# One recurrence for all four head pairs instead of two, and an output projection in one PSUM sum per tile

## The chip, the cores and the metric

The kernel runs on one core of a Trainium2 chip. The metric is the time of one execution on the device, in microseconds (us).

## The reference

One layer of a hybrid decoder: two SwiGLU feed-forward blocks, and between them a mixing layer of RWKV-7 heads beside a short convolution. A prompt of 512 tokens and 8 requests of 4 tokens go through it together.

```python
x = layer_norm(ALPHA * x + 0.5 * swiglu(x, ffn1...), ln1)
proj = x @ w_in                           # 3328 columns
r, k, v, wd, ad, gd = shift_mix(proj[:1792])
# 8 heads of 64; for each token
sa = S @ (-kk)
S  = S * w + outer(sa, kk * a) + outer(v, k)
o  = S @ r
y_rwkv = (group_norm(o) + sum(r * k * r_k) * v) * g
y_conv = c_b * conv3(c_c * c_h)
x = layer_norm(ALPHA * x + concat(y_rwkv, y_conv) @ w_out, ln2)
x = layer_norm(ALPHA * x + 0.5 * swiglu(x, ffn2...), ln3)
# outputs: x, and the last S, shift and conv rows of prompt and requests
```

## The kernel before, in words

**Layout.** Model dimensions lie on the 128 partitions, the T = 544 tokens (512 and 8 x 4) on the columns, cut into two halves of 256 and 288 (`HALF`). Each large product is made of three matmuls on split operands (`mm3`, lines L180, L181, L182); weights come from HBM as `raw` and are split into `hl` by ACT (L160) and DVE (L161).

**Fill.** The kernel records its instructions in one order by hand. Long products (input projection of the convolution, `conv`; output projection, `wout0`, `last0`, `wout1`) are generators in a background list, and `weave`, `slots`, `take` and `gap` put so many ns of them between the small matmuls of the recurrence. The table `FILL` gives those amounts. I call an L180/181/182 matmul in this part "fill". The order on each engine is thus fixed before it runs: an instruction that waits holds up everything behind it on its engine, and on the SP queue, which issues most of the DMAs.

**Recurrence.** The 8 heads are 4 pairs; two pairs are a group (g = 0: pairs 0 and 1, g = 1: pairs 2 and 3). The prompt is 8 chunks of 64 tokens, the requests are a ninth. For each pair, `scores` multiplies the scaled r, k, kk against each other (L1156) into `SC`, masks it (L1159), transposes what the chain needs and writes the matrix to be inverted to DRAM (`Ad`, L1163, SP). For each group:
- `elim(g)`: the 16x16 blocks on the diagonals are read back to the layout of one block per partition (`AT`, L1219), inverted on DVE in 15 steps of a multiply (L1230) and an add (L1232), written to DRAM (`Dd`, L1235 and L1236) and read back to the matmul layout (`DM` and `DT`, L1239). `DT` lies in `O`'s memory.
- `rounds(g)`: four rounds of 64-row matmuls (L1269) make the 64x64 inverses from the 16x16 ones.
- `chain(g)`: for chunk after chunk W (L1333, copied by ACT L1336), u (L1342), the state's product (L1351) with its update on DVE, and the outputs (L1312, L1318). The requests (`sample`: L1405, L1420, L1427, L1436, L1445) are put between.
- `gnorm(g, h)`: the norm of the outputs of a token half (L1463), gate (L1485).

The order in the program is scores of pairs 0 and 1, `elim(0)`, rounds, chain, norm; scores of 2 and 3, `elim(1)`, rounds, chain, norm. Group 0's result goes through DRAM (`ycd`).

**Output projection.** The sum over 8 blocks of 128 runs in two PSUM sums for the first token half: blocks 0, 1 and the convolution's 4 to 7 during chain 1 (`wout0`), blocks 2 and 3 behind it (`last0`), each added into `z` by DVE. The second half (`wout1`) has parts in one sum. Weights that both halves use are loaded and split twice.

**First layer norm.** The sums of squares over the 8 blocks are added by POOL for one token half (L344, L346; `add_sum`), the rest by DVE.

Of the kernel before, what the change touches and what calls it, by code (L numbers as in the profile page):

```python
# [67 lines left out]
FILL = dict(l1a=1.1, l1b=0.8, p0=11900, s0=0.93, p1=5506, s1=1.832, e0=0.658, c0=0.233, g0=0.399, g1=0.8, s2=0.531, p3=425, s3=0.85, e1=0.392, c1=0.963, c2=0.734, c3=0.8, l2a=0.94, l2b=1.25, l3a=0.88)  # L68
# [14 lines left out]
def body(ctx: ExitStack, tc: tile.TileContext, xT, gu1, wd1, win, wo_c, wo_0, wo_1, gu2, wd2, wl, ln3, eye, lora, vec, cst,  # L83
# [118 lines left out]
    def slots(gen, run):  # L202


        while True:
            with ExitStack() as st:
                if seen["fill"] is not None:
                    st.enter_context(tc.issue_after(seen["fill"].ins))
                if next(gen, None) is None:
                    break  # L210
            with ExitStack() as st:
                for e in [seen["pe"]] + seen["old"]:
                    st.enter_context(tc.issue_after(e.ins))
                take(run)
            seen["old"], seen["new"] = seen["new"], []
        seen["old"] = []
# [819 lines left out]
    SC = tl([P, 2, 2, NC_, P], F32, name="SC")  # L1036
    BK = tl([P, 2, 2, 8, 64], F32, name="BK")
    UV = tl([P, 2, 2, NC_, 64], F32, name="UV")
    XT = tl([P, NC_, 2, 64], F32, name="XT")
    DM = tl([P, NC_, 2, 64], F32, name="DM")  # L1040
    O = tl([P, 2, NC_, 64], F32, name="O")
    DT = O.rearrange("p a b t -> p (a b t)")[:, 0:1024].rearrange("p (c d t) -> p c d t", c=8, d=2)
    Pe = tl([P, 4, 8], F32, name="Pe")
    Pes = tl([P, 4, NSEQ], F32, name="Pes")
    ast = ExitStack()
    ARs = [(tl if g else pool(ast, "ar0").tile)([P, 2, NC_, 2, 64], F32, name=f"AR{g}") for g in (0, 1)]
    bvs = [[tl([P, 576], F32, name=f"bv{g}{pl}") for pl in range(2)] for g in range(2)]
    kfs = (kf, bvs[1][1]) * 2
    POOL.memset(bvs[1][1][:, T:576], 0.0)
    POOL.memset(XT, 0.0)  # L1050
    UP = tl([P, 2, 64], F32, name="UP")
    BS = tl([P, 2, P], F32, name="BS")
    POOL.memset(BS, 0.0)
    Ad = dr.tile([2, 16, 65, 64], F32, name="Ad")
    Dd = [dr.tile([2, 16, 65, 64], F32, name=f"Dd{i}") for i in range(2)]
    for d in Dd:
        for par in range(2):
            dma(d[par, :, 0:64].rearrange("c s t -> s c t"), XT[R(par), 0:8].rearrange("p c d t -> p (c d) t"))
    SEG = ((0, 256, 0), (256, 576, 1))

    class Pair:
# [79 lines left out]
        def scores(self):  # L1141
            p, pl, bkb, nk, vf = self.p, self.pl, self.bkb, self.nk, self.v

# [7 lines left out]
            AR, bv = ARs[p // 2], bvs[p // 2]  # L1151
# [13 lines left out]
            for a0c, n in ((0, 5), (5, 4)):  # L1165
# [8 lines left out]
                for par, q in enumerate(qs):  # L1174
                    src, dst = s64(q[:, :64 * m]), BK[:, pl, par, a0c:a0c + m, :]
                    if p == 2 and not a0c:
                        DVE.tensor_copy(dst, src)
                    else:
                        ACT.activation(dst, src, AF.Copy)
# [23 lines left out]
            for t0, t1, _ in SEG:  # L1203
# [3 lines left out]
                DVE.tensor_tensor(bv[pl][:, t0:t1], vf[:, t0:t1], q[:, :t1 - t0], op=OP.mult)  # L1207
# [4 lines left out]
    def elim(g, mid=None):  # L1212
        AR = ARs[g]
        est = ExitStack()
        ep = pool(est, f"elim{g}")
        AT = ep.tile([P, 16, 16], F32, name="AT")
        De = ep.tile([P, 16, 16], F32, name="De")
        tm = ep.tile([P, 64], F32, name="tm")
        dma(AT, diag(Ad))  # L1219
        POOL.memset(De, 0.0)  # L1220
        POOL.memset(De.rearrange("p a b -> p (a b)")[:, 0:256:17], 1.0)
        for pl in range(2):
            for par in range(2):
                sc = SC[R(par), pl, par, 0:8, 0:64]
                DVE.tensor_tensor(sc, sc, offm[R(par), None, :].to_broadcast([64, 8, 64]), op=OP.mult)
        yield 3000
        for k in range(15):
            n = 15 - k
            tv = tm[:, :n * (k + 1)].rearrange("p (i j) -> p i j", j=k + 1)
            DVE.tensor_tensor(tv, AT[:, k, k + 1:16, None].to_broadcast([P, n, k + 1]),  # L1230
                              De[:, k, None, 0:k + 1].to_broadcast([P, n, k + 1]), op=OP.mult)
# [5 lines left out]
        for d, x in zip(Dd, (DM[:, 0:8], DT)):  # L1237
            for par in range(2):
                dma(x[R(par)].rearrange("p c d t -> p (c d) t"), d[par, :, 0:64].rearrange("c s t -> s c t"))  # L1239
        est.close()  # L1240
        if mid is not None:
            mid()
        yield 24000 if g else 0

    def rounds(g):
        AR = ARs[g]
        pieces = (range(0, 4), range(4, 8), range(8, 9))
        for rnd in range(4):
            for x in pieces:
                sam = x[0] == 8  # L1250
                m = (64, 64, 32, 16)[rnd]
# [5 lines left out]
                for c in x:  # L1257
                    for pl in range(2):
                        for par in range(2):
# [3 lines left out]
                            lhs = DM[pr, c, pl, 0:m] if rnd else SC[pr, pl, par, c, 0:m]  # L1263
                            rhs = (DM if rnd == 0 else DT if rnd == 1 else XT) if not sam else XT
                            if sam and rnd < 2:
                                rhs = ident[pr, 0:32]
                            else:
                                rhs = rhs[pr, c, pl, j0:j0 + nn]
# [3 lines left out]
                if rnd == 0:  # L1272
                    for pr in (slice(0, 32), slice(64, 96)) if sam else (slice(0, P),):
                        ACT.activation(DM[pr, cc, :, 0:nn], qv[pr], AF.Copy)
                    continue
                elif rnd == 1 and not sam:
                    DVE.tensor_copy(XT[:, cc, :, 0:16], DT[:, cc, :, 0:16])
                    DVE.tensor_tensor(XT[:, cc, :, 16:64], qv, DT[:, cc, :, 16:64], op=OP.add)
                    continue
                for par in range(2):  # L1280
                    pr = slice(64 * par, 64 * par + m)
                    dst = XT[pr, cc, :, j0:j0 + nn]
# [6 lines left out]
            if rnd == 0:  # L1289
                for pl in range(2):  # L1290
                    for par in range(2):
                        POOL.tensor_copy(SC[R(par), pl, par, 0:8, 0:64], AR[R(par), pl, 0:8, 0, :])
# [5 lines left out]
    def chain(g, cp, small):  # L1298
# [3 lines left out]
        AR = ARs[g]  # L1302
        heads = [(pl, par) for pl in range(2) for par in range(2)]
        Ss, q2, uv = {}, None, []
# [4 lines left out]
        def out_u(c):  # L1309
            q = sm()  # L1310
            for pl, par in heads:
                crit(PE.matmul(at(q, pl, par), UV[:, pl, par, c, :], SC[:, pl, par, c, 64:128], start=(pl == 0 or c == 0),  # L1312
                               stop=(c == 0), skip_group_check=True))
            return q

        def out_s(c, q):
            for pl, par in heads if c else ():
                crit(PE.matmul(at(q, pl, par), Ss[c][R(par), pl, par, :], AR[R(par), pl, c, 1, :], start=False, stop=True,  # L1318
                               skip_group_check=True))
            o = ACT.activation(O[:, :, c, :], v2(q), AF.Copy)  # L1320
            for e in uv:
                after(o, e)

        for c in range(8):
            if c < 7:
                Sn = Ss[c + 1] = tl([P, 2, 2, 64], F32, name="S", bufs=3)
# [3 lines left out]
            q = sm()  # L1330
            for pl, par in heads:
                k = slice(0, P) if c else R(1 - par)
                crit(PE.matmul(at(q, pl, par), SC[k, pl, par, c, 0:64], Ss[c][:, pl, par, :] if c else UV[k, pl, par, c, :],  # L1333
                               start=True, stop=True))
            W = tl([P, 2, 64], F32, name="W", bufs=2)
            ACT.activation(W, v2(q), AF.Copy)  # L1336
            if c:
                q2 = out_u(c - 1)
            small(c, 0)
            qs = (sm(), sm())  # L1340
            for pl, par in heads:
                crit(PE.matmul(at(qs[par], pl, par), XT[R(par), c, pl, :], W[R(par), pl, :], start=True, stop=True))  # L1342
            seen["uv"] = DVE.tensor_copy(UV[R(0), :, 0, c, :], v2(qs[0], R(0)))
            seen["new"] = [ACT.copy(UV[R(1), :, 1, c, :], v2(qs[1], R(1)))]
            uv[:] = seen["new"]
            if c:
                out_s(c - 1, q2)
            small(c, 1)
            q = sm()
# [13 lines left out]
            if not g:  # L1363
                seen["step"] = upd, uv[0]
            small(c, 2)
            if c == 7:
                dma(wkvp_o[:, 2 * g:2 * g + 2, :], SF)
                out_s(7, out_u(7))
            yield 1

    def recur(g, cp, run):
        sam, gn = sample(g, cp), gnorm(g, 0, cp)
        first = (2, 2) if g else (1, 1)
        when = {first: 1, (2, 0): 1, (2, 1): 1, (3, 0): 1, (3, 1): 1, (4, 2): 1, (5, 2): 2, (6 if g else 7, 2): 2}

        gaps = {(0, 0): 600, (0, 1): 600, (1, 1): 300, (4, 0): 300, (4, 1): 300, (7, 0): 300, (7, 1): 300}

        def small(c, k):
            for _ in range(when.get((c, k), 0)):
                next(sam, None)  # L1380
            if (c, k) in gaps:
                gap(gaps[c, k])
            if (c, k) in ((5, 0), (5, 1), (6, 0)):
                next(gn, None)

        seen["fine"] = True
        slots(chain(g, cp, small), run)
        seen["fine"] = False
        for x in (sam, gn):
            for _ in x:  # L1390
# [513 lines left out]
```

## Time and profile before

| | |
|---|---|
| time, median of 3 runs | 1051.78 us (1051.11 to 1053.48) |
| the profiled execution's own time | 1052.82 us |
| its span, first to last instruction | 1051.1 us |
| PE busy | 1036.1 us of the span |
| DVE busy | 842.7 us |
| ACT busy | 602.5 us |
| POOL busy | 161.0 us |
| mean granted TensorE clock | 0.997 |

Matmuls are pipelined, so their durations overlap: a row's duration is from start to end of one (280 to 290 ns for a fill matmul), and what it costs the engine is the distance from its start to the next start. The trace has two records for one of the recurrence's 32-bit matmuls, which the program order lists once; counts below are those of the trace unless they are called the order's.

### The profile page before, as it was taken

The page shows a single profiled execution, that of the slowest core. Times are in us where ns is not written, and L with a number is a line of the kernel's source. Part 1 is how long each engine was busy: PE and PEld are TensorE (multiplying, and loading weights), DVE is VectorE, ACT ScalarE, POOL GpSimd, SP SyncE. Part 2 cuts the span into 40 slices and gives each one's busy share as a digit, 9 for nine tenths or more (in the row PEclk, how much of TensorE's full clock was granted, in tenths as well). Part 3 has the DMA queues.
Part 4 walks back from the last instruction along what each step waited for, and adds up shares of the span by engine and source line. Part 5 has one row for each costly group of instructions (what it writes and reads, how often), then busy time and mean ns, then how long its engine had stood idle before and what let it go on. Part 6 is the DMA issues. An engine that isn't in the chain of part 4 may idle for free.

```text
span 1051.1 us, 22674 instructions
## 1 busy us (share of the span) xinstructions
PE 1036.1 (99%) x9162; PEld 1004.3 (96%) x9162; DVE 842.7 (80%) x1521; ACT 602.5 (57%) x1155; POOL 161.0 (15%) x279
## 2 busy tenths in 40 slices
PE   9999999999999999999999999999999999999997
PEld 8999999999999899899889988999999999999995
DVE  6897988889775886896587668999889798897656
ACT  5765656565553569655454544677566565565514
POOL 0211111212100222123000200002112121120000
PEclk9999999999999999999999999999999999999999
DMA  8556676766745133325135744334667767686512
GB/s 295 137 135 148 152 183 149 163 161 152 171 120 162 61 106 94 95 73 122 43 106 168 176 127 147 131 120 99 144 161 161 162 142 175 148 180 162 141 44 85
DMA packets 91529, 144.49 MB, mean 137 GB/s; under 512 B 34848, under 2 KB 52384, under 8 KB 91296
## 3 DMA queue, kind: packets, MB, share of 16 engines
q1 hardware_dynamic: 68144, 110.76, 34.5%
q0 software_dynamic: 22848, 31.72, 19.4%
q8 instruction: 72, 1.18, 0.5%
q10 hardware_dynamic: 432, 0.56, 0.2%
q14 instruction: 33, 0.27, 0.1%
HBM read 128.81 MB, written 9.75 MB: 132 GB/s over the span
## 4 chain that ended last, share of the span: by engine, by line
PE 92%; DVE 5%; ACT 2%; DMA 1%; issue 1%; ACTq 0%; DVEq 0%
PE mm L623 10%; PE mm L619 10%; PE mm L622 10%; PE mm L180 9%; PE mm L181 8%; PE mm L182 8%; PE sm L623 7%; PE sm L619 7%; PE sm L622 7%; PE sm L507 1%; PE sm L1269 1%; PE mm L868 1%; DVE hl L161 1%; PE sm L832 1%; PE mm L832 1%; PE mm L507 1%
## 5 line engine op out<-in xcount | busy, mean ns | idle before, releaser
L180 PE MATMUL mm<-xhl,hl 128*128 128x288 f32 (+1 forms) x704 | 209.0, 299 | 0.4 <-DVE z L1682 0.4
L404 DVE TENSOR_TENSOR hl<-raw,hl 128x1024 fp32r<-128x1024 f32 x156 | 187.6, 1220 | 22.8 <-ACT hl L401 20.8
L181 PE MATMUL mm<-xhl,hl 128*128 128x288 f32 (+1 forms) x704 | 203.0, 289 | 0.9 <-DVE xhl L169 0.9
L182 PE MATMUL mm<-xhl,hl 128*128 128x288 f32 (+1 forms) x704 | 202.2, 288 | 0.0
L401 ACT ACTIVATE hl<-raw 128x1024 fp32r<-128x1024 f32 x156 | 162.2, 1054 | 59.5 <-DVE raw L404 54.2
L180 PEld LDWEIGHTS mm<-xhl,hl 128*128 128x128 f32 x704 | 132.2, 189 | 7.1 <-issue 1.6
L181 PEld LDWEIGHTS mm<-xhl,hl 128*128 128x128 f32 x704 | 132.8, 189 | 2.6 <-DVE xhl L169 1.1
L182 PEld LDWEIGHTS mm<-xhl,hl 128*128 128x128 f32 x704 | 132.7, 189 | 0.1
L623 PE MATMUL sm<-xhl,hl 128*128 128x272 f32 x432 | 124.6, 289 | 0.0
L619 PE MATMUL sm<-xhl,hl 128*128 128x272 f32 x432 | 124.3, 288 | 0.0
L622 PE MATMUL sm<-xhl,hl 128*128 128x272 f32 x432 | 124.3, 288 | 0.0
L161 DVE TENSOR_TENSOR hl<-raw,hl 128x1024 fp32r<-128x1024 f32 (+3 forms) x74 | 80.9, 1106 | 9.6 <-ACT hl L160 9.2
L623 PE MATMUL mm<-tv,hl 128*128 128x272 f32 x288 | 83.3, 289 | 0.0
L622 PE MATMUL mm<-tv,hl 128*128 128x272 f32 x288 | 83.0, 288 | 0.0
L619 PE MATMUL mm<-tv,hl 128*128 128x272 f32 x288 | 82.5, 286 | 0.0
L160 ACT ACTIVATE hl<-raw 128x1024 fp32r<-128x1024 f32 (+3 forms) x74 | 68.6, 944 | 22.9 <-PE mm L182 10.4
L622 PEld LDWEIGHTS sm<-xhl,hl 128*128 128x128 f32 x432 | 81.3, 188 | 0.0
L619 PEld LDWEIGHTS sm<-xhl,hl 128*128 128x128 f32 x432 | 81.2, 188 | 0.0
L623 PEld LDWEIGHTS sm<-xhl,hl 128*128 128x128 f32 x432 | 81.1, 188 | 0.0
L610 POOL DMA_DIRECT2D raw<-in_gu x36 | 47.6, 1324 | 203.5 <-DVE hlb L404 127.4
L610 POOL DMA_DIRECT2D raw<-in_wd x32 | 39.3, 1483 | 248.8 <-DVE hlb L404 163.4
L404 DVE TENSOR_TENSOR raw<-raw 128x512 f32<-128x512 f32 x104 | 71.7, 689 | 2.3
(438 smaller groups left out, 2806.1 us busy)
## 6 DMA issues: line engine op xcount, KB each, us to landing
raw<-in_gu SPq DMA_DIRECT2D x84, 512.0 KB, 4.9
raw<-in_gu POOLq DMA_DIRECT2D x36, 512.0 KB, 6.5
raw<-in_wd SPq DMA_DIRECT2D x32, 512.0 KB, 4.4
raw<-in_win SPq DMA_DIRECT2D x26, 512.0 KB, 3.9
raw<-in_wd POOLq DMA_DIRECT2D x32, 256.0 KB, 5.9
z<-sv POOLq DMA_DIRECT2D x16, 272.0 KB, 7.4
raw<-in_wo_c SPq DMA_DIRECT2D x8, 512.0 KB, 4.7
raw<-in_wd SPq DMA_DIRECT2D x8, 384.0 KB, 3.2
```

What stands on the lines that cost most here:

```text
L160: seen["hi"] = ACT.activation(hl[:, 0, a:b], raw[:, a:b], AF.Copy)
L161: seen["lo"] = DVE.tensor_tensor(hl[:, 1, a:b], raw[:, a:b], hl[:, 0, a:b].bitcast(F32), op=OP.subtract)
L180: PE.matmul(out, wh, src[:, 0, k, c0:c1], start=(start and i == 0), stop=False)
L181: PE.matmul(out, wh, src[:, 1, k, c0:c1], start=False, stop=False)
L182: seen["fill"] = PE.matmul(out, wl, src[:, 0, k, c0:c1], start=False, stop=(stop and i == n - 1))
L401: return self.link(0, ACT.activation(*args, **kw))
L404: return self.link(1, DVE.tensor_tensor(out, a, b, op=op))
L507: PE.matmul(o[i][h][:, :c1 - c0], block(hl, v, k), xhl[:, y, k, c0:c1], start=(k == 0 and j == 0), stop=(k == KD - 1 and j == 2), skip_gro ...
L610: POOL.dma_start(dst.rearrange("p (s c) -> p s c", s=2), bass.AP(tensor=a11.tensor, offset=a11.offset, ap=[[row, P], [P * row, 2], [1, 512 ...
L619: e = PE.matmul(out, wh, src(0, i), start=(first and i == 0), stop=False, skip_group_check=True)
L622: PE.matmul(out, wh, src(1, i), start=False, stop=False, skip_group_check=True)
L623: self.pe = PE.matmul(out, wl, src(0, i), start=False, stop=(i == n - 1), skip_group_check=True)
```

## The change

- Scores of all four pairs come first. One `elim` inverts the blocks of both groups: the same 15 steps, each on [128, 2, ...] (L1234, L1236 of the changed kernel), with one `AT`/`De` pair of tiles for both, and two sets of DRAM tiles (`Ad0`, `Ad1`, `Dd00` to `Dd11`).
- One `rounds` does both groups in turns, with no fill in between (`r=0`).
- One `chain` does both groups in turns: in each of 8 steps w of group 0, state of group 1, output, u of group 0, and the same with the groups exchanged, then one run of fill. Both `sample`s and the norm of the first token half are put between.
- `z` is scratch memory during the recurrence and is loaded afterwards (`zload`). Projections behind the chain sum all 8 blocks in PSUM (`wout(h)`), each weight is loaded once, and one DVE operation scales and adds. The norm of the second half is woven into `wout(0)`.
- The bonus term (r k r_k v) goes to DRAM (`bvd`, SP) and is read back in `gnorm`.
- `add_sum` is always on DVE. Pair 2's copy of `BK` is on ACT. The fourth convolution tile is made by `conv` as the others are.

```diff
-FILL = dict(l1a=1.1, l1b=0.8, p0=11900, s0=0.93, p1=5506, s1=1.832, e0=0.658, c0=0.233, g0=0.399, g1=0.8, s2=0.531, p3=425, s3=0.85, e1=0.392, c1=0.963, c2=0.734, c3=0.8, l2a=0.94, l2b=1.25, l3a=0.88)
+FILL = dict(l1a=1.1, l1b=0.8, p0=11900, s0=0.93, p1=7280, s1=1.832, p2=5500, s2=1.8, p3=5500, s3=1.7, e=0.72, r=0, c=8000, g=2.4, l2a=1.2, l2b=1.25, l3a=0.88)
...
     def add_sum(s1, z, d, c0, c1, off=False):
         n = c1 - c0
-        eng = POOL if off and d < KD - 1 else DVE
+        eng = DVE
...
-                DVE.tensor_tensor(bv[pl][:, t0:t1], vf[:, t0:t1], q[:, :t1 - t0], op=OP.mult)
+                DVE.tensor_tensor(nk[:, t0:t1], vf[:, t0:t1], q[:, :t1 - t0], op=OP.mult)
+            dma(bvd[p], nk[:, 0:T])
...
-            DVE.tensor_tensor(De[:, k + 1:16, 0:k + 1], De[:, k + 1:16, 0:k + 1], tv, op=OP.add)
-            yield 400
-        DVE.tensor_copy(AT, De.rearrange("p a b -> p b a"))
-        dma(diag(Dd[0]), De)
-        dma(diag(Dd[1]), AT)
+            DVE.tensor_tensor(lower, lower, tv, op=OP.add)
+            yield 500
+        DVE.tensor_copy(AT, De.rearrange("p g a b -> p g b a"))
+        for g in range(2):
+            dma(diag(Dds[g][0]), De[:, g])
+            dma(diag(Dds[g][1]), AT[:, g])
...
+        for c in range(8):
+            w_part(0, c)
+            if c:
+                s_part(1, c - 1)
+                out_u(0, c - 1)
+            small(c, 0)
+            u_part(0, c)
+            if c:
+                out_s(0, c - 1)
+            w_part(1, c)
+            small(c, 1)
+            s_part(0, c)
+            if c:
+                out_u(1, c - 1)
+            u_part(1, c)
+            if c:
+                out_s(1, c - 1)
+            small(c, 2)
             yield 1
...
+    weave("e", elim())
...
+    slots(chain(cp, small), lambda: max(0, conv_left[0] - FILL["c"]) / next(steps_left))
...
+                yield from mm3(o[:, :n], wo[0, d // 4], xhl, (0, 1), c0, c1, (d % 4) * 2, start=False, stop=False)
+            yield from mm3(o[:, :n], wo[1, d // 4], xhl, (2, 3), c0, c1, (d % 4) * 2, start=False)
```

What this does to the SP queue around the block inverse: before, `elim(1)`'s stretch reads so (the last write of scores to `Ad` stands two rows ahead of it).

```order
L1219 DMA AT_7211<-Ad_4733 128x16x16
L1649 DMA y_7356<-ycd_73 128x544
L1649 DMA y_7358<-ycd_73 128x544
L1664 DMA z_7198<-xsp_72 128x1088 x4
L975 DMA raw_7505<-in_win 128x1024
L1534 DMA ycd_73<-zc_6823 128x544
L1235 DMA Dd0_4734<-De_7212 128x16x16
L1236 DMA Dd1_4735<-AT_7211 128x16x16
L1239 DMA DM_4715<-Dd0_4734 64x16x64 x2
L1239 DMA O_4716<-Dd1_4735 64x16x64 x2
```

In the changed kernel the same place on SP reads as follows (`DMs` lie in `z`, `nk` holds the bonus of pair 3).

```order
L1207 DMA bvd_4733<-nk_5949 128x544
L975 DMA raw_6505<-in_win 128x1024
L1220 DMA AT_6218<-Ad0_4727 128x16x16
L1220 DMA AT_6218<-Ad1_4728 128x16x16
L1240 DMA Dd00_4729<-De_6219 128x16x16
L1241 DMA Dd01_4730<-AT_6218 128x16x16
L1240 DMA Dd10_4731<-De_6219 128x16x16
L1241 DMA Dd11_4732<-AT_6218 128x16x16
L1245 DMA z_6208<-Dd00_4729 64x16x64 x2
L1245 DMA z_6208<-Dd10_4731 64x16x64 x2
L1245 DMA DT0_6216<-Dd01_4730 64x16x64 x2
L1245 DMA DT1_6217<-Dd11_4732 64x16x64 x2
```

The read of the blocks now stands behind two DMAs that wait for DVE (the bonus product of pair 3, and the split that frees a `raw` buffer), and four writes stand ahead of the first read-back.

The chain on PE before, one step of group 0 (step 4; a run of fill is shown by its first matmuls):

```order
L1333 MATMUL sm_6462<-S_6394,SC_4711 64x64 x4
L1312 MATMUL sm_6469<-SC_4711,UV_4713 64x64 x4
L180 MATMUL mm_6384<-xhl_68,hl_6239 128x256
L181 MATMUL mm_6384<-xhl_68,hl_6239 128x256
L182 MATMUL mm_6384<-xhl_68,hl_6239 128x256
L1342 MATMUL sm_6478<-W_6467,XT_4714 64x64
L1318 MATMUL sm_6469<-AR0_4722,S_6318 64x64 x4
L180 MATMUL mm_6496<-xhl_68,hl_6239 128x288
L1351 MATMUL sm_6500<-UV_4713,BK_4712 64x64 x4
L1436 MATMUL sm_6509<-SC_4711,UV_4713 64x64 x4
```

The chain on PE in the changed kernel, step 5 of both groups (L1323 is w, L1332 u, L1340 the state, L1360 and L1366 the outputs, L1447 a request's update):

```order
L1323 MATMUL sm_7558<-S0_7426,SC_4718 64x64 x4
L1340 MATMUL sm_7472<-UV_4720,BK_4719 64x64 x4
L1360 MATMUL sm_7573<-SC_4718,UV_4720 64x64 x4
L1447 MATMUL sm_7488<-ux_7489,BS_4722 128x512
L1332 MATMUL sm_7558<-W0_7563,z_6208 64x64 x4
L1366 MATMUL sm_7573<-AR0_4713,S0_7286 64x64 x4
L1323 MATMUL sm_7601<-S1_7469,SC_4718 64x64 x4
L1360 MATMUL sm_7625<-SC_4718,UV_4720 64x64 x4
L1340 MATMUL sm_7558<-UV_4720,BK_4719 64x64 x4
L1332 MATMUL sm_7601<-W1_7606,z_6208 64x64 x4
L1366 MATMUL sm_7625<-AR1_4714,S1_7329 64x64 x4
L180 MATMUL mm_7545<-xhl_68,hl_7386 128x288
```

Where three runs of fill stood within a step of one group, one of 30 to 33 matmuls now stands behind a step of both. By the program's order, PE goes from small matmuls to fill and back 49 times between the first round and the end of the norms before, and 18 times now. In the rounds, fill stood behind each round of a group; in the changed kernel 192 fill matmuls stand between the last matmul of scores and the first of the rounds, and then all 288 (of the order) of the rounds without any. First come 16 of group 0, and the next is one of group 1.

## Rows read from the trace of the kernel before

**Rows 1.** The page: PE's busy time in the span.

```profile
PE 1036.1 (99%) x9162; PEld 1004.3 (96%) x9162; DVE 842.7 (80%) x1521; ACT 602.5 (57%) x1155; POOL 161.0 (15%) x279
```

**Rows 2.** Windows: busy of PE, PEld, DVE, ACT, POOL (instructions), clock, DMA.

```profile
484.58:541.90 57.32, 56.74 (x886) 48.66 (x884) 37.49 (x101) 24.25 (x67) 11.33 (x31) 1.00 0.21 65
566.06:595.36 29.30, 29.30 (x237) 29.30 (x235) 20.74 (x63) 15.35 (x28) 4.13 (x16) 1.00 0.98 252
595.36:653.28 57.92, 56.44 (x892) 49.44 (x892) 41.64 (x102) 27.24 (x69) 5.12 (x12) 0.97 0.38 120
653.28:697.00 43.72, 43.34 (x338) 42.60 (x337) 42.37 (x74) 28.53 (x48) 0.00 (x0) 1.00 0.42 143
```

**Rows 3.** The same windows, the matmuls of L180 alone on PE.

```profile
484.58:541.90 57.32, 18.82 (x56) 1.00 0.21 65
566.06:595.36 29.30, 22.33 (x78) 1.00 0.98 252
595.36:653.28 57.92, 19.45 (x59) 0.97 0.38 120
```

**Rows 4.** Timeline of PE in chain 1: start, duration, instruction, idle before and releaser.

```profile
607.21 0.28 PE L182 MATMUL mm<-xhl,hl 128*128 128x256 f32 x1
607.42 0.45 PE L1342 MATMUL sm<-W,XT 64*64 64x64 f32 x8
607.80 0.39 PE L180 MATMUL mm<-xhl,hl 128*128 128x256 f32 x1
608.03 0.29 PE L181 MATMUL mm<-xhl,hl 128*128 128x256 f32 x1
...
610.70 0.45 PE L1333 MATMUL sm<-S,SC 128*64 128x64 f32 x8
610.98 0.40 PE L1312 MATMUL sm<-SC,UV 128*64 128x64 f32 x8
611.56 0.45 PE L1342 MATMUL sm<-W,XT 64*64 64x64 f32 x8 [0.17 <-ACT W L1336]
```

**Rows 5.** Windows: two stretches of rounds 0 (L1269 alone), one of chain 1.

```profile
484.58:486.83 2.25, 2.25 (x72) 2.04 (x72) 2.22 (x6) 0.97 (x2) 2.05 (x6) 1.00 0.59 172
489.42:493.00 3.58, 3.56 (x132) 3.21 (x132) 2.21 (x6) 0.26 (x1) 3.05 (x8) 1.00 0.00 0
618.14:621.21 3.07, 3.07 (x23) 2.92 (x18) 1.23 (x5) 0.43 (x2) 0.00 (x0) 0.61 0.61 212
```

**Rows 6.** Timeline of the SP queue around `elim(1)`.

```profile
560.76 1.26 SPq L1163 DMA_DIRECT2D Ad<-SC  x2
...
564.53 0.38 SPq L1219 DMA_DIRECT2D AT<-Ad  x1
...
579.81 0.37 SPq L1235 DMA_DIRECT2D Dd<-De  x1
...
585.58 1.31 SPq L1239 DMA_DIRECT2D DM<-Dd  x2
```

**Rows 7.** The tile AT: DMA issue to landing; Dd: the same.

```profile
DMA to landing us min/median/max: 4.0/4.8/6.8
...
DMA to landing us min/median/max: 3.3/4.6/6.8
```

**Rows 8.** Groups by line on DVE between 569.4 and 580.0 us (last figure: mean ns | idle).

```profile
L1232 DVE TENSOR_TENSOR De<-De,tm 128x15 f32<-128x15 f32 (+7 forms) x15 | 3.1, 208 | 0.4
L1230 DVE TENSOR_TENSOR tm<-AT,De 128x15 f32<-128x15 f32 (+7 forms) x15 | 3.1, 203 | 0.4
...
L161 DVE TENSOR_TENSOR hl<-raw,hl 128x1024 fp32r<-128x1024 f32 x1 | 1.2, 1226 | 0.0
```

**Rows 9.** Timeline of POOL and of DVE in the first layer norm.

```profile
353.70 1.13 POOL L346 TENSOR_TENSOR cpb<-cpb,z 128x288 f32<-128x288 f32 x1 [1.06 <-DVE z L495]
...
354.08 1.83 DVE L161 TENSOR_TENSOR hl<-raw,hl 128x1024 fp32r<-128x1024 f32 x1
...
356.44 0.44 DVE L495 TENSOR_TENSOR z<-z,sm 128x288 f32<-128x288 f32 x1
```

More of the change, by code (lines that the diff above doesn't have):

```diff
@@ L1175, in scores @@
                     src, dst = s64(q[:, :64 * m]), BK[:, pl, par, a0c:a0c + m, :]
[L1176 to L1179, printed above, removed]
+                    ACT.activation(dst, src, AF.Copy)
                     if a0c:
@@ L1296, in v2, with chain, w_part @@
         return q[rows, :128].rearrange("p (d t) -> p d t", d=2)
-    def chain(g, cp, small):
+    def chain(cp, small):
         tl = cp.tile
-        AR = ARs[g]
         heads = [(pl, par) for pl in range(2) for par in range(2)]
-        Ss, q2, uv = {}, None, []
+        Ss, bank, outq, uv = [{}, {}], {}, {}, {}
         def at(q, pl, par):
             return q[R(par), pl * 64:pl * 64 + 64]
[L1309 to L1324, printed above, removed]
+        def w_part(g, c):
+            SC, UV = SCs[g], UVs[g]
             if c < 7:
-                Sn = Ss[c + 1] = tl([P, 2, 2, 64], F32, name="S", bufs=3)
+                Sn = Ss[g][c + 1] = tl([P, 2, 2, 64], F32, name=f"S{g}", bufs=3)
                 with tc.issue_after(seen["pool"].ins):
@@ L1362, in chain, with out_u @@
             seen["new"].append(upd)
-            if not g:
-                seen["step"] = upd, uv[0]
-            small(c, 2)
+            seen["step"] = upd, uv[g]
             if c == 7:
                 dma(wkvp_o[:, 2 * g:2 * g + 2, :], SF)
-                out_s(7, out_u(7))
-            yield 1
[L1371 to L1390, printed above, removed]
-                pass
+        def out_u(g, c):
+            SC, UV = SCs[g], UVs[g]
+            outq[g] = sm()
+            for pl, par in heads:
+                crit(PE.matmul(at(outq[g], pl, par), UV[:, pl, par, c, :], SC[:, pl, par, c, 64:128], start=(pl == 0 or c == 0),
+                               stop=(c == 0), skip_group_check=True))
@@ new lines, in out_s @@
+        def out_s(g, c):
+            q = outq[g]
+            for pl, par in heads if c else ():
+                crit(PE.matmul(at(q, pl, par), Ss[g][c][R(par), pl, par, :], ARs[g][R(par), pl, c, 1, :], start=False, stop=True,
+                               skip_group_check=True))
+            o = ACT.activation(Os[g][:, :, c, :], v2(q), AF.Copy)
+            after(o, uv[g])
+        for c in range(8):
[16 more added lines that the diff above has]
+            small(c, 2)
+            yield 1
@@ L1599, in body, with counted @@
     pairs[0].prep(kf, rf, vf)
-    cv = seq(*(conv(i) for i in range(3)))
-    bg.extend((own_a(1), cv))
+    fin, cdone = [], []
+    CONV = 4 * 3 * 24 * (T / 2.4 + 6)
+    conv_left = [CONV]
+    def counted(gen):
+        for need in gen:
+            conv_left[0] -= need
+            yield need
+    bg.extend((own_a(1), counted(seq(*(conv(i) for i in range(4))))))
     take(FILL["p0"])
@@ L1604, in body @@
     need(1, 1)
-    bg.extendleft((own_a(2), own_b(1)))
-    take(FILL["p1"])
-    need(1, 2)
-    weave("s1", pairs[1].scores())
-    need(2, 1)
-    bg.appendleft(own_b(2))
-    def pair3():
-        need(2, 2)
-        bg.appendleft(own_a(3))
-        need(3, 1)
-    weave("e0", elim(0, pair3))
-    cst0 = ExitStack()
-    cp = pool(cst0, "chain0")
-    slots(rounds(0), 600)
-    recur(0, cp, 1100)
-    seen["step"] = None
-    weave("g0", gnorm(0, 1, cp))
-    cst0.close()
-    ast.close()
@@ L1626, in body @@
-    w4 = pool(ast, "w4")
-    wstate["ex_hl"] = [lambda: w4.tile([P, 2, 1024], F32R, name="hl", bufs=1)]
-    weave("s2", pairs[2].scores())
-    bg.appendleft(own_b(3))
-    need(3, 2)
-    take(FILL["p3"])
-    weave("s3", pairs[3].scores())
+    for p in range(1, 4):
+        bg.extendleft((own_a(p + 1), own_b(p)) if p < 3 else (own_b(p),))
+        take(FILL[f"p{p}"])
+        need(p, 2)
+        weave(f"s{p}", pairs[p].scores())
+        if p < 3:
+            need(p + 1, 1)
     prs.close()
@@ L1711, in last0 @@
-    def last0():
-        c0, c1 = HALF[0]
-        for d in range(KD):
-            if d % 4 == 0:
-                w1s[d // 4] = wload(wo_1[d // 4])
-                wstate["pin"].add(wstate["last"])
-                wstate["hl"] = 0 if d else 4
-            e = d % 2
-            if not e:
-                o = big()
-            yield from mm3(o[:, e * c1:e * c1 + c1], w1s[d // 4], xhl, (2, 3), c0, c1, (d % 4) * 2)
-            if e:
-                add_z(d - 1, 0, o, 2)
-                for x in (d - 1, d):
-                    add_sum(f2.s1[0], z, x, c0, c1)
-            yield 6 * 120
@@ new lines, in slot, with ysplit @@
+    def slot(p, par):
+        return SC[:, p, par, 0:4, :].rearrange("p c t -> p (c t)")
+    sams = [sample(g, cp) for g in (0, 1)]
+    gns = []
+    for g in range(2):
+        ps_ = (2 * g, 2 * g + 1)
+        gns.append(gnorm(g, 0, [slot(p, 1)[:, 0:256] for p in ps_],
+                         [cp.tile([P, 2, 256], F32R, name=f"gh{p}") for p in ps_],
+                         [slot(p, 1)[:, 256:512] for p in ps_], [slot(p, 0)[:, 0:256] for p in ps_]))
+    def ysplit(k, y, c0, c1, d0):
+        split(xhl[:, 0, k, c0:c1], xhl[:, 1, k, c0:c1], y[:, c0 - d0:c1 - d0])
@@ new lines, in body @@
+    seen["fine"] = True
+    steps_left = iter(range(8, 0, -1))
+    slots(chain(cp, small), lambda: max(0, conv_left[0] - FILL["c"]) / next(steps_left))
+    seen["fine"] = False
+    until(lambda: fin)
+    for x in sams + [ysg] + gns:
+        for _ in x:
+            pass
+    drain()
+    seen["step"] = None
+    cst1.close()
+    mbs.close()
+    pst = ExitStack()
+    wop = pp = pool(pst, "post")
+    y1 = {k: pp.tile([P, 288], F32, name=f"y{k}") for k in (4, 5, 6)}
+    lnq = pp.tile([P, KD, 288], F32, name="lnq")
```

463 lines of the change are left out of this document (226 added, 237 removed).

## The prediction

> **What bounds the kernel now.** I read the page first: PE is busy for 1036.1 of 1051.1 us [rows 1], so the kernel is bound by PE, and a change gains only where PE spends time on something other than matmuls at full pace, or loses where PE has to wait. The windows show where that is. In the dense stretch from 566.06, 234 fill matmuls (78 of each of three lines) take 29.30 us, 0.125 us each, with nothing lost [rows 2, 3]. The two stretches that hold rounds, chain and norm of one group do not look like that: 57.32 us with 168 fill matmuls, and 57.92 us with 177. At 0.125 us the fill is worth 21.0 and 22.1 us, so the recurrence itself costs PE 36.3 and 35.8 us, 72.1 together [rows 2, 3]. PE still counts as busy there, because the durations of pipelined matmuls overlap; the reader must look at starts. The timeline shows what the 72 us hold besides work: every change of kind costs. From a fill matmul to a small group 0.21 us passes, the group takes 0.38 up to the next fill, and that first fill another 0.23: 0.82 in all [rows 4]. Two fill matmuls in a dense run take 0.25 and a small group that is followed by another small one 0.28 (610.70 to 610.98), so a return trip costs 0.82 - 0.53 = 0.29 us. The rest is waiting, as the 0.17 us for ACT's copy of W at 611.56 [rows 4], and one stretch at a lower clock [rows 5].
>
> **The change, term by term.** *Fewer trips.* The matmuls are the same ones; the order has 18 returns to fill where it had 49. 31 x 0.29 = 9.0 us gained. With 0.2 (the two changes into and out of fill at their shortest, an estimate from the same starts) and 0.35 as ends this is 6 to 11.
>
> *Waits in the chain.* Before, W's copy needed about 0.17 us more than the one group behind w covers [rows 4]. Now the other group's state and output (two groups, 2 x 0.28) stand there, which is enough. In its place comes the wait of group 1's w for the state update on DVE that starts four groups earlier; by the same 0.28 a group that is about a wait's width short, some 0.2 to 0.4 us in each of 8 steps. No row of before shows this pairing. Nothing gained is one end, 5 us gained the other (waits gone); I take 1.4 gained, since the single-group chain waits in every step too and has the norm's groups and the request's updates between.
>
> *The block inverse.* This is where something is late. Before, the read of the blocks (`AT`) was issued at 564.53, 1.5 us ahead of the dense run of fill; the last DVE step ended at 579.81, the read-back began at 585.58 [rows 6], and landed about 4.6 us after its issue [rows 7], at 590.2 to 591. Rounds began at 595.36, where the dense window ends: hidden, with 4 to 5 us over. In the changed kernel PE has 192 fill matmuls between scores and rounds, 24.0 us. I count from the start of that run. On SP, `AT` now stands behind `bvd`, which waits for DVE's two bonus products, at about 1.3 us (0.44 each for 128x288 [rows 9], and the pipeline), and behind a weight load that waits for a 1.23 us split [rows 8] to free its buffer: issue at 3.5, against -1.5 before. Landing takes 4.8 [rows 7], somewhat more for two reads: 8.8. The 30 DVE operations took 0.205 us at 15 to 64 elements and have twice as many now. By the DVE rows (0.44 for 288 elements, 0.205 for some 45) that adds 0.05, and with a gap of some 0.03 they need 8.4 us; a split of 1.23 and an operation of 256 elements between them add 1.6 [rows 8, 9]: inverse done at 19 (before: 13.7). From there to the first read-back was 5.8 us, so 24.5 now, and landing at 29 to 30. PE arrives at 24.0 and waits 5.5 us. Behind the first 32 matmuls (of the trace) of group 0 stands one of group 1, whose read-back is two issues later: another 1 us. I take 6.5. Ends: 2 (`bvd` and the split early, landings at the shortest, 3.3) and 11 (landings at the longest, 6.8, twice, with four writes in the queue instead of two).
>
> *The clock after that wait.* Granted clock fell once before, to 0.61 in the window at 618.14, where 23 fill records took 3.07 us instead of some 1.9 [rows 5]; PE had only small matmuls ahead of it. Rounds, all small matmuls, kept the full clock at 489.42 [rows 5]. After 6 us without any matmul I expect 1.2 GHz at the start of the rounds. With the fall lasting about as long as that one, and the loss there of 1.1 us in 3.07, doubled because the small matmuls may not count as well as fill, this costs 2.0; ends 0 and 8 (all the rounds at half the clock). The Trainium skill, "TensorE: Matmul & The Clock Gate", section "HAM oscillation — how this bites in real kernels", speaks against the change here: a PE that waits for DMA in the middle of its work falls back to half the clock and starts the next burst cold. The one fall at 618.14 came without such a wait, so this trace neither shows nor refutes it.
>
> *The adds that leave POOL.* At 354.08, beside a POOL add that runs from 353.70 to 354.83, DVE's split takes 1.83 us; alone it takes 1.23 [rows 8, 9]. With six such adds DVE loses up to 6 x 0.6 = 3.6 us; the six adds on DVE cost 6 x 0.44 = 2.6. Ends: 1 us lost, 2.5 gained (the whole of what PE waits there); I take 0.5 gained. In the Trainium skill's "SBUF — State Buffer", section "SBUF: two separate sides", a DVE operation with two SBUF inputs and a GpSimd operation that reads SBUF take a shared port pair in turn, for a whole instruction each; the 0.60 us by which the split is longer agree with that, being most of the add's remaining 0.75.
>
> *Edits at nothing.* Weights loaded once (six splits fewer on DVE and ACT), one DVE operation for scale and add, `BK` on ACT: engines off the path. The projections behind the chain are the exception: in 653.28 to 697.00 DVE is busy 42.37 of 43.72 us already [rows 2], so the norms and splits there are covered by fill only just. I take 0; if cover is gone, up to 3 us. Bonus tiles come back by DMA long before use. Scores of pairs 2 and 3 have the same matmuls as before with more fill between: 0.
>
> *Sum.* -9.0 - 1.4 + 6.5 + 2.0 - 0.5 = -2.4 us. The profiled execution took 1052.82 us, so 1050.4; the median of the runs is 1.04 lower, so that I forecast 1049.4 against 1051.78. With the bounds taken as independent the forecast's own range is 1044 to 1055.
>
> **Rivals.** *A, the inverse stays hidden.* For it: 4 to 5 us were left over before [rows 6, 7]. Against it: the SP order, where `AT` cannot be issued before the bonus product. Then the wait and the clock's fall go: -10.9, 1040.9.
>
> *B, the clock stays down (slower).* The wait puts PE at 1.2 GHz, and rounds and chain clusters, which have small matmuls alone for 3 to 15 us, don't bring it back. For it: the fall at 618.14 behind small matmuls. Against: 489.42, at full clock [rows 5]. The price: fill there went at 3.07/1.9, 1.6 times as long; both groups' rounds are about 14 us (3.58 us for 132 of 576, the first ones slower [rows 5]), so 0.6 x 14 = 8.4 in place of 2.0, then one fall of 1.1 us at half of the 8 clusters: -2.4 + 6.4 + 4.4 = +8.4, 1060. It decides from 5 us at the low clock on.
>
> *C, the chain does not gain.* Group 1's state update comes late by a whole DVE pass, as fill's splits (1.23 us each) stand between on DVE: 8 x 0.8 = 6.4 us more than I took: +4.0, 1055.8. For it: DVE is 65 to 72% busy in those stretches [rows 2]. Against it: the same splits stood there before.
>
> *D, the change does nothing to PE:* trips cost less than I count, or are replaced by the same waits; -9.0 becomes 6 and the wait for the inverse is as counted: +0.6, 1052.4.
>
> **How the numbers follow.** Forecast 0.45, A 0.17, B 0.12, C 0.13, D 0.13. A difference of 0.2%, 2.1 us, is about what a measurement of this kernel can tell from none. The forecast at -2.4 with its spread is faster in six parts of ten, the same in three and slower in one: 0.27, 0.13, 0.05. A is faster; B and C are slower; D is the same in eight of ten parts (0.10), the rest split. Faster 0.27 + 0.17 + 0.01 = 0.45; same 0.23; slower 0.32. The range must reach A at one end and C, with a part of B, at the other: 1040 to 1057.
>
> **What would show each step.** Trips: the stretch from rounds to the last norm, less its fill at 0.125, falls from 72 to about 62 us, waits for the inverse apart. Inverse: an idle PE of 5 to 8 us ahead of the first L1274, with a DMA read of `Dd00` as releaser, and `AT` issued 3 to 4 us after the fill run begins. Clock: a granted clock under 1 in the rounds, for 3 to 7 us. Adds: no DVE split over 1.3 us between 351 and 367. I am wrong if PE does not wait ahead of the rounds, if the clock is down in the chain, or if PE waits for DVE in the projections.

## The result, and the profile after

The changed kernel takes 1055.7 us (median of 12 runs, 1052.0 to 1058.48) where the kernel before takes 1052.51 (12 runs): a ratio of 1.0025, with an interval of 1.0014 to 1.0035. It is slower by a quarter of a per cent; the forecast was 1049.4, faster. The time is within the range, on the other side of no change. One execution of e_more, below, took 2499.18 us and is left out of that run's figures.

The profiled execution is the slowest of the twelve, 1058.48 us with a span of 1056.7, 5.66 us longer than the profiled one of before. Its windows from the last fill ahead of the rounds on (columns as in [rows 2]):

```profile
498.71:522.70 23.99, 23.99 (x195) 23.99 (x193) 16.49 (x47) 5.02 (x8) 3.41 (x10) 1.00 0.55 116
527.59:551.35 23.76, 20.25 (x592) 19.20 (x592) 8.42 (x28) 5.73 (x17) 10.44 (x28) 0.72 0.65 95
551.35:572.44 21.09, 21.09 (x252) 20.03 (x251) 6.52 (x16) 5.75 (x16) 0.00 (x0) 0.70 0.26 87
572.44:629.52 57.08, 56.35 (x817) 48.88 (x815) 45.19 (x120) 28.63 (x86) 7.71 (x22) 1.00 0.35 115
629.52:664.01 34.49, 32.60 (x264) 31.71 (x261) 28.77 (x64) 18.00 (x39) 0.00 (x0) 1.00 0.67 222
```

The third figure from the end, the mean granted clock, is the reading that matters: 0.72 in the rounds and 0.70 in the chain's first two steps. The records have two levels, 2.4 GHz (1.00) and 1.2 GHz; a mean between them is made of both, and I call a stretch at the lower one a fall. In [rows 2] the same work had 1.00 and 0.97. The 4.9 us between the first window and the second are PE waiting, as its timeline shows at the start of the rounds:

```profile
527.73 0.47 PE L1274 MATMUL sm<-z,SC 64*64 64x64 f32 x2 [4.79 <-DMA z<-Dd]
529.29 3.92 PE L1274 MATMUL sm<-z,SC 64*64 64x64 f32 x66 [1.09 <-DMA z<-Dd]
...
537.94 1.33 PE L1274 MATMUL sm<-DT,z 64*64 64x48 f32 x36 [1.33 <-DMA DT<-Dd]
...
540.69 3.64 PE L1274 MATMUL sm<-DT,z 64*64 64x48 f32 x60
```

4.79 + 1.09 + 1.33 = 7.2 us of waiting for the read-backs of the inverse. The first 66 records behind it took 3.92 us, where 64 of the same kind and 8 more took 2.25 in [rows 5]: 1.2 GHz.

What led to the wait stands on SP (the queue of [rows 6]):

```profile
499.61 0.33 SPq L1207 DMA_DIRECT2D bvd<-nk  x1
501.31 0.33 SPq L975 DMA_DIRECT2D raw<-in_win  x1
501.69 3.02 SPq L1220 DMA_DIRECT2D AT<-Ad  x2
...
517.81 0.38 SPq L1240 DMA_DIRECT2D Dd<-De  x1
...
522.26 4.79 SPq L1245 DMA_DIRECT2D z<-Dd  x4
```

Counted from the start of the fill run at 498.71, the read of the blocks is issued at 3.0, the inverse is done at 19.1, and its read-back begins at 23.6. In the first layer norm, by line on DVE between 351 and 367 us, the split is back at its own length (compare [rows 9]) and the adds stand there instead:

```profile
L161 DVE TENSOR_TENSOR hl<-raw,hl 128x1024 fp32r<-128x1024 f32 x5 | 6.1, 1218 | 0.0
...
L346 DVE TENSOR_TENSOR cpb<-cpb,z 128x288 f32<-128x288 f32 x5 | 2.3, 452 | 0.0
```

Behind the chain PE waits again, for the norm of the second half, woven into the projection:

```profile
PE sm L1462 <- ACT gq L1484: 1.4, 1, 1.4
```

The twelve runs differ mainly in the clock: 1052.0 us at a mean granted clock of 0.993, 1058.48 at 0.985. A straight line through the twelve gives 0.79 us for each 0.001, and 1048.5 us at 0.998, which is the mean of the kernel before in the runs beside the experiments. That is an estimate by extrapolation, not a run: by it, some 7 us of the median are the clock's.

### The profile page after: what moved, and what is told of

The parts are those of the page before. It is cut to its first block, busy times and chain, and to the rows that moved or that the text cites. A ratio compares the mean times of both kernels' runs of the same rounds, so it can differ in the third digit from the quotient of the medians.

```text
span 1056.7 us, 22648 instructions
## 1 busy us (share of the span) xinstructions
PE 1034.1 (98%) x9162; PEld 1008.1 (95%) x9162; DVE 830.0 (79%) x1485; ACT 594.0 (56%) x1149; POOL 159.4 (15%) x273
## 4 chain that ended last, share of the span: by engine, by line
PE 88%; DVE 5%; ACT 3%; DMA 2%; SPq 1%; issue 1%; ACTq 0%; POOL 0%; DVEq 0%
PE mm L623 10%; PE mm L619 10%; PE mm L622 10%; PE mm L180 7%; PE sm L623 7%; PE sm L619 7%; PE sm L622 7%; PE mm L181 7%; PE mm L182 7%; PE sm L507 1%; PE sm L1274 1%; PE mm L832 1%; PE sm L832 1%; PE mm L868 1%; PE mm L507 1%
## 5 line engine op out<-in xcount | busy, mean ns | idle before, releaser
L180 PE MATMUL mm<-xhl,hl 128*128 128x256 f32 (+1 forms) x624 | 182.6, 295 | 1.2 <-ACT xhl L168 1.2
L181 PE MATMUL mm<-xhl,hl 128*128 128x256 f32 (+1 forms) x624 | 180.8, 291 | 0.1
L182 PE MATMUL mm<-xhl,hl 128*128 128x256 f32 (+1 forms) x624 | 180.2, 290 | 0.0
L180 PEld LDWEIGHTS mm<-xhl,hl 128*128 128x128 f32 x624 | 118.7, 191 | 5.0 <-ACT xhl L168 1.4
L181 PEld LDWEIGHTS mm<-xhl,hl 128*128 128x128 f32 x624 | 119.0, 191 | 0.6 <-DVE xhl L169 0.4
L182 PEld LDWEIGHTS mm<-xhl,hl 128*128 128x128 f32 x624 | 118.7, 191 | 0.2 <-DVE hl L161 0.2
L161 DVE TENSOR_TENSOR hl<-raw,hl 128x1024 fp32r<-128x1024 f32 (+3 forms) x63 | 65.7, 1059 | 8.6 <-ACT hl L160 8.3
L160 ACT ACTIVATE hl<-raw 128x1024 fp32r<-128x1024 f32 (+3 forms) x63 | 57.4, 926 | 19.4 <-PE mm L182 9.6
```

Of the source, the lines that this page charges most:

```text
L160: seen["hi"] = ACT.activation(hl[:, 0, a:b], raw[:, a:b], AF.Copy)
L161: seen["lo"] = DVE.tensor_tensor(hl[:, 1, a:b], raw[:, a:b], hl[:, 0, a:b].bitcast(F32), op=OP.subtract)
L180: PE.matmul(out, wh, src[:, 0, k, c0:c1], start=(start and i == 0), stop=False)
L181: PE.matmul(out, wh, src[:, 1, k, c0:c1], start=False, stop=False)
L182: seen["fill"] = PE.matmul(out, wl, src[:, 0, k, c0:c1], start=False, stop=(stop and i == n - 1))
```

## The experiments

Two theories of the low clock were set against each other. **W**: the wait ahead of the rounds brings it down, and the later falls follow from that. **S**: the rounds and the first steps, which are nearly all small matmuls, bring it down, whatever is ahead of them. Each kernel is the changed one, or the one before, with the edit shown. All ratios are to the kernel before.

**Cover ahead of the rounds** (e_more).

```diff
-e=0.72
+e=1.35
```

> Cover for the inverse: FILL e from 0.72 to 1.35, so that 264 fill matmuls stand ahead of the rounds instead of 192, taken from the runs in the chain. 72 x 0.125 = 9.0 us more work ahead of the rounds, against 7.2 us that PE waited for DMA there. Theory W (the wait brings the clock down, and the falls behind it follow from that): no wait of more than 0.5 us ahead of the first matmul of the rounds, full clock in the rounds, at most one fall in the chain; 7 us of wait and some 8 us of clock back: 1040 to 1044. Rival S (the rounds bring the clock down, because 288 small matmuls stand together without fill, whatever is ahead of them): the wait goes, the falls in rounds and chain stay: 1047 to 1050.

Measured: 1051.02 us, ratio 0.9984 (0.9969 to 0.9999). The wait ahead of the rounds is gone, but the time is in neither theory's range. Windows of its profile, rounds first:

```profile
532.01:552.44 20.43, 17.10 (x610) 15.85 (x608) 8.32 (x29) 6.10 (x18) 10.42 (x28) 0.90 0.53 96
552.44:572.29 19.85, 18.34 (x340) 16.77 (x338) 10.53 (x30) 7.10 (x21) 2.64 (x6) 0.93 0.24 89
```

And what PE waited for in the whole of it:

```profile
PE sm L1274 <- issue: 1.9, 2, 1.3
PE mm L182 <- DVE hl L161: 1.5, 1, 1.5
...
PE sm L1274 <- DMA DT<-Dd: 1.2, 2, 0.6
PE sm L1323 <- DVE S L1350: 1.0, 1, 1.0
```

The clock fell without any wait ahead of the rounds, so W as it stands does not hold; the mean clock of the runs is 0.9926 against 0.9894 in the changed kernel, so the wait had a part. But there were waits inside the rounds, and the fall (from 548.3) begins in the longest of them:

```profile
549.04 0.93 PE L1274 MATMUL sm<-z 64*16 64x16 f32 x55 [1.34 <-issue]
```

So this run does not show that small matmuls alone bring the clock down, as S has it. And 7.2 us of waiting became 1.2 for `DT` and 1.9 without a releaser in the rounds, 1.0 for the state in the chain, and 1.5 for a weight split in the fill of its step 0: work moved ahead of one wait is missing at the next.

**Fill inside the rounds, wait left** (r600).

```diff
-r=0
+r=600
```

> Fill inside the rounds: FILL r from 0 to 600, four runs of 6 to 12 fill matmuls between the rounds, the wait ahead of the rounds left as it is. Theory W: the wait of 6 to 7 us and the low clock behind it stay, the clock comes back a little sooner at best, and four returns to fill cost 1.2 us: 1054 to 1057. Rival S: the rounds are no longer a long stretch of small matmuls, so that the clock is up from the first run of fill on: 1048 to 1051.

Measured: 1051.15 us, ratio 0.9987 (0.9975 to 0.9999). The wait is still 5.9 us. The clock is below full in the rounds' window alone, and full from the chain's start on, where the changed kernel had 0.70:

```profile
526.92:549.11 22.19, 20.06 (x598) 18.84 (x600) 7.13 (x24) 5.78 (x16) 10.41 (x28) 0.85 0.71 116
549.11:571.00 21.89, 21.75 (x408) 20.24 (x401) 10.88 (x36) 7.85 (x25) 1.31 (x7) 1.00 0.23 71
```

The time is S's, within 0.2 us, though with a low clock behind the wait as W has it. In this profile one fall stands behind the wait and there is no other. It is the fastest of the eleven runs, 1049.47 us at a clock of 0.994; the mean of all is 0.9926, so others can have had more falls.

**Both** (e_more_r600).

> Both: more cover ahead of the rounds and fill inside them. Theory W: as with cover alone, with 1.2 us for four more returns to fill: 1041 to 1045. Rival S: only now are the rounds at full clock: 5 us or more below the run with cover alone.

Measured: 1048.8 us, ratio 0.9961 (0.9946 to 0.9976), mean clock 0.995. The lowest median of the study (its interval overlaps with that of e_r, below), and 2.2 us below cover alone: less than the 5 us that S asked for, in the direction of S. Its profile still has 0.84 and 0.85 in the windows of rounds and steps 0 and 1, at 1049.3 us of span; the fastest of its runs, 1045.45, had 0.998.

**Adds back on POOL** (adds_pool).

```diff
-        eng = DVE
+        eng = POOL if off and d < KD - 1 else DVE
```

> The first layer norm's adds back on POOL, all else as in the changed kernel. I had counted 0.5 us for this term, with 2.5 as an end; the windows of both traces from 352.7 to 375 have PE 1.9 us short of busy before and 0 after. If that is the adds' work: 1.9 us slower than the changed kernel. If it is something else: no difference, and PE has no gap between 353 and 367.

Measured: 1057.44 us, ratio 1.0051 (1.0028 to 1.0074), 1.7 us above the changed kernel, with intervals that overlap: alone it does not show a difference. Its window of the layer norm has PE 1.9 us short of busy:

```profile
353.00:375.00 22.00, 20.08 (x154) 19.30 (x153) 21.78 (x31) 14.54 (x27) 6.70 (x9) 1.00 0.29 96
```

**The adds on DVE in the kernel before** (b_adds), the same line the other way round.

> The kernel before with nothing changed but the first layer norm's adds on DVE. By the run with the adds back on POOL (1.7 us slower than the changed kernel, with wide intervals) and by the windows: 1.9 us faster than before, 1051.3, and PE busy throughout 353 to 367.

Measured: 1051.1 us, ratio 0.9989 (0.998 to 0.9998): 1.2 us faster by the ratio, 1.7 by the medians, and the gap is gone. The same window, the kernel before first:

```profile
352.70:375.00 22.30, 20.38 (x156) 19.61 (x155) 22.08 (x32) 15.27 (x28) 6.60 (x8) 1.00 0.29 95
...
352.70:375.00 22.30, 22.30 (x179) 22.24 (x178) 21.43 (x39) 16.25 (x30) 0.69 (x5) 1.00 0.28 95
```

The gain is 1.2 to 1.7 us by this run, and 1.9 by the window; adds_pool points the same way.

**Fill between the requests' products** (gaps).

```diff
+    GAPS = ((1, 0), (1, 1), (2, 0))
...
+        if (c, k) in GAPS:
+            gap(700)
```

> The changed kernel with three runs of 9 fill matmuls inside the chain's steps 1 and 2, behind the requests' products (L1407), taken from the runs behind the steps; wait and rounds as they are. Theory S (stretches of small matmuls bring the clock down wherever they stand): the fall in step 1 (563.9 in the changed kernel's profile) goes, worth about 2.5 us there, against three returns to fill at 0.29: 1054. Theory W (all falls follow from the wait): nothing gained, 1056.6.

Measured: 1054.93 us, ratio 1.0018 (1.0008 to 1.0028). The second window is what the edit aimed at, 0.92 where it was 0.70; the rounds ahead of it still have a low clock, 0.79:

```profile
527.00:551.00 24.00, 18.05 (x592) 16.87 (x592) 8.15 (x28) 5.88 (x17) 10.41 (x28) 0.79 0.72 119
551.00:574.00 23.00, 23.00 (x346) 21.35 (x345) 9.58 (x25) 6.80 (x19) 0.32 (x2) 0.92 0.18 60
```

The fall in step 1 is gone from this profile. All eleven runs have a clock of 0.990 to 0.992, where six of the changed kernel's twelve had 0.988 or less, so the low end is gone. On the median it gives 0.8 us, with intervals that overlap: the time alone does not tell S's 1.6 us from nothing. At the same clock (0.992) its runs are 0.8 us slower than the changed kernel's (five and four runs), near the 0.9 that three returns were to cost.

**A little cover and fill in the rounds** (e_r: e 1.1, r 600), and the same **with the runs inside steps 1 and 2** (e_r_gaps).

> Cover ahead of the rounds at 228 fill matmuls (FILL e 1.1) and fill inside the rounds (r 600). Against 264 and 600 (1048.8) some 2.7 us of wait are left ahead of the rounds, and as much fill is given back to the chain and the projections. Theory S: a fall behind the short wait is ended by the first fill: 1047 to 1050. Theory W: the short wait does not bring the clock down: same, but without any fall in the rounds.

> The run before with the three runs of fill inside steps 1 and 2 as well. Theory S: full clock from the rounds to the end in most executions, 0.996 or more on the mean: 1045 to 1047, and a narrower spread of times. Theory W: 0.9 us slower than without those runs.

Measured: 1049.5 us, ratio 0.9973 (0.9964 to 0.9983), and 1049.39, ratio 0.9971 (0.9958 to 0.9983). The second has a mean clock of 0.997, against 0.995 without those runs, and no better time. Three more returns at 0.29 us would explain that, but no run separates the two. e_r's profiled execution was at full clock throughout the recurrence:

```profile
528.19:551.18 22.99, 18.61 (x598) 16.97 (x600) 7.67 (x25) 5.27 (x15) 10.43 (x28) 1.00 0.68 108
```

4.4 us of this window PE is not busy: 3.0 us of waits for read-backs, the longest of them below, and 1.2 without a releaser are now inside the rounds, and no fall came behind them.

```profile
529.89 1.14 PE L1274 MATMUL sm<-z,SC 64*64 64x64 f32 x30 [1.23 <-DMA z<-Dd]
```

**A run of fill behind each half step** (half), on e_r.

```diff
                 out_s(0, c - 1)
+            yield 1
             w_part(1, c)
...
-    steps_left = iter(range(8, 0, -1))
+    steps_left = iter(range(16, 0, -1))
```

> The kernel with cover 228 and fill in the rounds (e_r, 1049.5), its chain with a run of fill behind each half step (one group's turn) in place of each whole step: 15 runs of 12 where there were 8 of 24. By my price of a return to fill (0.29 us) 7 more cost 2.0 us: 1051.5. Rival: the fill hides the wait of a group's w for its state update, which I had priced at 0.2 to 0.4 us a step, and the stretches of small matmuls are half as long, so that the clock stays up: 1047 to 1049.

Measured: 1053.49 us, ratio 1.0002 (0.9993 to 1.0011), 4.0 us above e_r. The rival is out: more and shorter runs cost. Of runs at the same clock (0.998), one of each, the difference is 1051.11 - 1048.35 = 2.8 us, 0.39 us for each of 7 more returns; at 0.995, with three and four runs, it is 3.8 us. That is no smaller than my price, but it has more in it than the returns. One run of fill waits for a weight split, and the clock falls there:

```profile
559.41 0.58 PE L182 MATMUL mm<-xhl,hl 128*128 128x256 f32 x1 [1.47 <-DVE hl L161]
```

Shorter clusters did not hold the clock up either (mean 0.994).

**Less cover** (e_less: e 0.3).

> Less cover: FILL e from 0.72 to 0.3, 120 fill matmuls ahead of the rounds instead of 192, the 72 given to the chain's runs. More cover had given back less than the wait it took away. If fill in the chain is pure work (it hides nothing there): the wait grows by 9.0 to 16 us and the time by as much, 1064.5. If fill in the chain hides waits of the chain or the projections, as I now think: the time grows by 5 to 7 us only, 1061 to 1063. In theory W the clock is lower than in the changed kernel (mean under 0.989), in S not (more fill in the chain).

Measured: 1065.13 us, ratio 1.0124 (1.011 to 1.0139): 9.4 us above the changed kernel, and not the 5 to 7 that I thought. The wait for the first read-back is 12.9 us where it was 4.8. The mean clock is 0.987, lower than with the shorter wait, as W has it. By the line through the twelve runs that is some 1.7 of the 9.4 us, which leaves 7.7 for 9.0 us of fill: in the chain it hides little. What cover did not give back (e_more) is in part seen in that run's waits, two of them in the chain.

**No fill in the rounds of the kernel before** (b_r0).

```diff
-    slots(rounds(0), 600)
+    slots(rounds(0), 0)
...
-    slots(rounds(1), 600)
+    slots(rounds(1), 0)
```

> The kernel before with no fill inside its two sets of rounds, no wait ahead of them. Theory S: stretches of some 8 us of small matmuls bring the clock down without any wait: mean clock 0.996 or less, 1053 to 1056. Theory W: clock as before (0.998), eight returns to fill saved (2.3 us), copies between the rounds uncovered (about 1 us): 1051 to 1052.

Measured: 1057.14 us, ratio 1.0035 (1.0023 to 1.0047), at a mean clock of 0.998. The time is in neither theory's range; on the clock W was right and S was not. Two sets of rounds, 8.8 and 7.6 us of small matmuls with no wait over 0.4 us among them, kept the full clock. In the profile, the fastest of the five runs, the time went elsewhere, to a stretch behind the last norm where DVE is busy throughout and PE waits 1.4 us for its adds into `z` (L1682) and 1.4 for weight splits:

```profile
484.70:493.49 8.79, 8.19 (x289) 7.33 (x288) 7.61 (x20) 2.86 (x8) 7.78 (x17) 1.00 0.02 4
...
649.38:659.71 10.33, 7.95 (x55) 7.01 (x55) 10.02 (x21) 4.07 (x8) 0.00 (x0) 1.00 0.87 303
```

54 fill matmuls took 10.3 us there, 3.6 more than their pace. That the fill left out of the rounds is what is missing here is argued, not shown.

**Twice the fill in the rounds, little cover** (e9_r1200: e 0.9, r 1200).

> Cover 204 matmuls and twice as much fill inside the rounds (FILL e 0.9, r 1200), where PE still waited for read-backs and copies. If those waits are what is left: 1.5 us below e_r, 1048. If the wait ahead of the rounds (5 us of it left) counts as before: 1050 to 1052.

Measured: 1051.45 us, ratio 0.9987 (0.9978 to 0.9995). That is the second range: the wait ahead of the rounds (4.5 us left) counts, and no gain is seen from fill in the rounds beyond r 600. Cover and fill in the rounds changed together here, so the two are not told apart.

## Why the prediction was wrong

**The step that failed is the clock behind the wait.** I took 2.0 us, with 8 as an end, and priced the case that happened as rival B, 1060, at a chance of 0.12. In the profile the clock is at 0.72 and 0.70 for 45 us, with four falls where I had one. By the price of the matmuls behind the falls it cost some 10 us there: 66 records 3.92 us against 2.1 at full clock, 60 of the next kind 3.64 against 2.06 in e_more's profile, 96 of the kind after that 2.77 against 1.71 in that of gaps, the fill of steps 0 and 1 4.0 us above its pace, 32 of the requests' products 1.83 against 1.10, the rest in other groups of steps 0 and 1. The line through the twelve runs gives the same for this execution (1058.48 - 1048.5), and 7 for the median. Without the falls, that line has the kernel 4.0 us below the one before; the forecast less its clock term was 4.4 below.

**What brings the falls is open.** Rival B's mechanism was half of it. The first fall does stand behind the wait (here and in r600), and the wait and the missing fill together are worse than either alone (mean clock 0.9894, against 0.9926 in both e_more and r600). But neither W nor S covers the rest. In the fourteen profiles the clock falls 22 times, the end of the program apart. Shortly ahead of 18 of these falls, or as they begin, PE waits, 0.7 to 12.9 us at the longest; all falls in the rounds are of this kind. The other four stand in the chain behind the requests' products (L1407; L1405 in the kernel before, whose one fall is of this kind), with PE busy throughout. The small matmuls ahead of the changed kernel's fourth fall:

```profile
559.63:564.10 4.47, 4.47 (x123) 4.18 (x124) 1.09 (x5) 2.16 (x6) 0.00 (x0) 1.00 0.02 4
```

So a fall can come without any wait, while the rounds' matmuls alone (b_r0) brought none, and waits of up to 1.2 us among them (e_r) need not bring one. These are readings of one execution of each kernel, and no run varied the short waits or the requests' products alone. How the two causes share the 7 us is open too; e_more and r600 take back 4.7 and 4.5 us each, but each of these has the wait's or the returns' price in it as well.

Two readings in the prediction of this step were off and moved it little. Of the 23 records in the window at 618.14, 8 are of the state's product (L1351) and 15 are fill; the 1.9 us is right for the 15. And 3.58 us for 132 matmuls makes 15.6 us for the 576 of the rounds, not about 14.

**The wait** was right: `AT` issued at 3.0 us after the start of the fill run (3.5 predicted), inverse at 19.1 (19), read-back at 23.6 (24.5), wait 7.2 (6.5). The 30 DVE operations took 0.254 us each (0.255 worked out). Its parts fit less well: 4.8 us ahead of the first matmul and 1.1 ahead of group 1 are 5.9 of the 6.5, and the 1.3 us for `DT` was in no term. That the sums agree is partly luck.

**The adds** were mis-sized: 1.2 to 1.7 us gained by b_adds, not 0.5. I had set DVE's own time against DVE's own time; what counted was that PE waited in the kernel before, 0.9 and 0.2 us for splits on DVE (L169) and 0.8 for one on ACT (L168), and in the changed one not at all.

**Trips and waits in the chain** were too optimistic. From 527.59 to 664.01 the profile has 136.4 us; its fill (480 matmuls at 0.125) is 60.0, the waits for read-backs within it are 2.4 and the clock about 10. That leaves 64 us for what took 72.1 before, of which 1.1 was clock: 7 us gained, not 10.4. e_r's profile, at full clock, says 6: from 528.33 to the same place in the program, 653.10, it has 124.8 us, less 55.5 of fill (444 matmuls), 3.0 of waits for read-backs and 1.2 for its four more returns is 65. Where the rest of the 10.4 went is shown in part only: 1.4 us is the wait for the norm in the projection, an edit that I had put at 0 to 3, and 0.7 a wait of the first w. half gives no sign that a return costs less than the 0.29 us I took.

That rival C's time, 1055.8, is the one measured is luck: its wait, w for the state update on DVE, is not among the waits of the changed kernel's profile.

The sum by these terms for the profiled execution: -7 + 7.2 + 9 (10 less the fall of before) - 1.9 = +7, against 5.7 measured; some 1.5 us are not accounted for.

## What to carry to other kernels

Gathering the small matmuls saves returns to the long ones, but it also makes stretches without long ones, and the clock can fall in them: cost such a change with the whole of the gathered stretch at the low clock, and keep some long matmuls in it (r600, e_r). Look for waits among the small matmuls too: most falls here stood behind one. Two half-size latency chains in series can each be hidden behind the other's work; merged into one, the chain has all of the work in front of it or behind it, so check what the fill ahead of its result is worth against its length (24 us against 29 here). Fill that is moved to cover one wait is missing at the next: 7 us of wait taken away gave under 5 back.

## What the runs showed that I had not expected

One core's clock fell up to four times within 45 us, though PE was busy in most of it with small matmuls, while 8.8 us of the rounds' matmuls without fill, and with 0.6 us of waits in all, left it at 1.00 (b_r0). The kernel before had such a fall as well, behind the requests' products. Executions of one and the same program differed by 6.5 us with it (1052.0 at 0.993, 1058.48 at 0.985), so a single profile of such a kernel may show either end.
